# The loads of an inverse's 16x16 blocks, moved from ScalarE's queue to SyncE's and spread over units of dense products

## The chip, the cores and the metric

One NeuronCore of one Trainium2 chip runs the whole kernel. The engines are TensorE (PE in the profile; PEld is its weight load), VectorE (DVE), ScalarE (ACT), GpSimd (POOL) and SyncE (SP); each works through its own instruction queue in order, and DMAs are issued from the queues of SyncE and ScalarE. The metric is the device time of one execution in microseconds (us), lower is better.

## The reference

A decoder trunk of two layers on 256 tokens of width 2048. In each layer the normalised input goes through one wide input projection, whose columns feed two groups of heads: a gated DeltaNet (8 heads) and an HGRN2 recurrence (8 heads). Both outputs are joined, projected back and added; then a gated layer embedding is added.

```python
hn = rms_norm(h, norm_w[l])
proj = hn @ w_in[l]
...
y_a = deltanet_branch(dn_qkv, dn_z, dn_b, dn_a, ...)
y_b = hgrn2_branch(hg_q, hg_f, hg_i, hg_z, ...)
h = h + jnp.concatenate([y_a, y_b], axis=-1) @ w_out[l]
gate = jax.nn.sigmoid(h @ w_ple_gate[l])
h = h + (p[l] @ w_ple_up[l]) * gate
```

The DeltaNet needs, per head and chunk, a triangular system to be solved:

```python
A = jnp.where(strict, jnp.einsum("bhncd,bhnsd->bhncs", k_beta, k) * decay, 0.0)
sol = lax.linalg.triangular_solve(A + eye, rhs, left_side=True, lower=True, unit_diagonal=True)
```

The change touches only how the inverse of that unit triangular matrix is brought together.

## The kernel before

**Dense products.** Every projection runs as a sequence of steps. A step takes a block of weights of 512 KB (in0, in1, out, gate and up in the profile; the digit is the layer), multiplies both halves of the tokens with it, and ends with a call of `tick()`. One such step is a unit. Weights are f32 and are split into a high and a low part, with three matmuls for each product: `raw` is loaded by SyncE (line 378), ScalarE makes the high part `whi` (line 400), VectorE subtracts to get the low part `wlo` (line 402). There are three raw buffers (`WRAW = 3`) and three of each part. `ahead(n)` issues loads up to four steps ahead and splits up to two steps ahead of step n. The order of TensorE's instructions is that of the program text; the framework may shift instructions of the other engines against each other.

**Everything else is generators.** The work on heads is written as generators that are resumed by `tick()`: `yield self.wait(x)` lets so many units pass, `yield self.after(x)` or a lambda waits for a condition. How many units each wait takes stands in the tables `DELAY` (by kind: "d" DeltaNet group, "i" inverse, "h" HGRN2 group, "b" what follows the output and gate products) and `DELAY_AT` (for one group or layer: `d3c` is group 3's wait `c`, `i0t16` layer 0's wait `t16`). There are four groups of two heads each; in the profile dn03 is layer 0's DeltaNet group 3, hg11 layer 1's HGRN2 group 1. When a chunk of the input projection ends, ScalarE copies its PSUM bank with the row factor (`evict`, line 597, for instance hg01fqet), and a generator goes on from there. The dense products have three PSUM banks, a chunk uses two.

**The inverse** (class `Inverse`, di0 and di1 in the profile) does all 16 matrices of a layer at once, when the last of four groups has given its part (`given`). It clears the result `Tt` on GpSimd, collects the 16x16 diagonal blocks through DRAM with one matrix per partition, and inverts them with 15 short steps on VectorE (lines 653 and 656). Then ScalarE writes them to the DRAM scratch `d2` (line 658), two units pass (`w`), and eight loads of 16 KB each bring the blocks to the diagonals of `Tt` (line 662), one for each block row. After a further wait (`T`) VectorE transposes blocks of 32 (line 671), and three rounds of small TensorE products with copies between them join blocks of 16, 32 and 64 into one of 128, each round behind waits of its own (`t16`, `p16`, `t32`, `p32`, `t64`, `p64`; VectorE lines 690, 695, 718 to 721, ScalarE lines 681, 704, 712, 731, 740). At the end `ready` is set; the DeltaNet groups wait for it before `z0` and then multiply with `Tt`. The lines that the change touches:

```python
nc.scalar.dma_start(out=d2.rearrange("(q a c) -> q a c", q=128, a=16), in_=X)
yield self.wait("w")
for j in range(8):
    b = slice(16 * j, 16 * j + 16)
    nc.scalar.dma_start(out=Tt[b, :, b], in_=d2.rearrange("(i b a c) -> b a i c", i=NT, b=8, a=16)[j])
yield self.wait("T")
```

Of the kernel before, what the change touches and what calls it, by code (L numbers as in the profile page):

```python
# [15 lines left out]
DEPTH, D, T, KT = 2, 2048, 256, 16  # L16
# [15 lines left out]
def chunk_cols(chunk):  # L32

    return [(START[k], 16) if k == "ba" else (START[k] + 256 * g, 256) for k, g in chunk]
# [2 lines left out]

DELAY = {
    "d": {'c': 1, 'D': 4, 'k': 6, 'q': 7, 'ssq': 1, 'v': 5, 'z0': 1, 'S': 1, 'w': 1, 'z1': 1, 'o': 1, 'y': 3, 'yp': 1},
    "i": {'F': 4, 'F2': 1, 'F3': 1, 'F4': 1, 'w': 2, 'T': 6, 't16': 3, 'p16': 2, 't32': 3, 'p32': 2, 't64': 3, 'p64': 2},  # L40
    "b": {'o': 1, 'g': 4},
    "h": {'c': 1, 'f': 1, 'x2': 1, 'x4': 1, 'x8': 1, 'a': 2, 'x16': 1, 'x32': 1, 'x64': 1, 'u16': 2, 'u64': 1, 'o': 2, 'y': 2, 'yp': 1, 'q': 0},
}
# [1 line left out]
DELAY_AT = {  # L45
    "b1g": 5,
    "d0q": 6, "d0y": 2, "d0z1": 2,
    "d2D": 3, "d2k": 4, "d2o": 2, "d2q": 9, "d2y": 2,
    "d3D": 5, "d3ssq": 3,
    "h0o": 4, "h0u16": 1, "h0u64": 3, "h0y": 3, "h0yp": 2,  # L50
    "h1c": 3, "h1o": 1, "h1q": 1, "h1x32": 3, "h1x8": 3, "h1yp": 4,
    "h2c": 2, "h2f": 2, "h2q": 2,
    "h3u64": 2, "h3x2": 2,
    "i0p16": 1, "i0t16": 5,
    "i1t16": 2,
# [111 lines left out]
def trunk(ctx: ExitStack, tc: tile.TileContext, head, xT, x, pT, W, par, fw, cst, msk, eye, out):  # L167
    nc = tc.nc
# [113 lines left out]
    d2 = dr.tile([256 * 128], F32, name="d2")  # L282
# [20 lines left out]
    def bc1(ap, n):  # L303
        return ap.unsqueeze(1).to_broadcast([ap.shape[0], n, ap.shape[1]])
# [259 lines left out]
    def mix(tag, n, bufs, name):  # L564
        return mp.tile([128, n], F32, tag=tag, name=name, bufs=bufs)

    def v4(ap):
        return ap.rearrange("p (a b) -> p a b", b=128)
# [43 lines left out]
    class Inverse:  # L612


        NT = 4 * NG
# [21 lines left out]
        def run(self):  # L637
            n, Bt, NT = self.n, self.Bt, self.NT


            Tt = self.Tt = v4(mix("Tt", 128 * NT, 1, n + "Tt"))
# [3 lines left out]
            F, X = fx[:, 0], fx[:, 1]  # L645
# [3 lines left out]
            for c in range(1, 16):  # L649
# [3 lines left out]
                i = V.tensor_tensor(pr_[:, :c, :c], X[:, :c, :c], bc1(F[:, :c, c], c), ALU.mult)  # L653
# [5 lines left out]
            yield self.wait("w")  # L659
            for j in range(8):  # L660
                b = slice(16 * j, 16 * j + 16)
                nc.scalar.dma_start(out=Tt[b, :, b], in_=d2.rearrange("(i b a c) -> b a i c", i=NT, b=8, a=16)[j])
            yield self.wait("T")


# [4 lines left out]
            for b in blocks:  # L670
                i = V.transpose(Tn[b:b + 32], Tt[b:b + 32, :, b:b + 32])
# [52 lines left out]
            for i in range(NT):  # L724
                for b in (64, 96):
                    c = 64 * (i % 8)
# [7 lines left out]
            for i in range(NT):  # L734
                for b in (0, 32):
                    c = 64 * (i % 8)
# [520 lines left out]
    for l in range(DEPTH):  # L1257
# [25 lines left out]
        for c, k4 in order:  # L1283
# [5 lines left out]
            w = 2 if sum(n for _, n in chunk_cols(ch)) > 272 else 4  # L1289
# [114 lines left out]
```

## Time and profile before

| | |
|---|---|
| median of 3 runs | 1256.43 us (1256.11 to 1256.9) |
| the profiled execution | 1256.09 us |
| its span, first to last instruction | 1254.4 us |
| mean granted TensorE clock | 0.995 |
| waits of SyncE's queue for wlo before a weight load | 815.2 us, 299 times |

The difference of 1.7 us between the profiled execution's time and its span lies before the first and behind the last instruction. In the rows of the trace, times are us from the span's start, durations of single instructions us or, in groups, busy us and mean ns of one; a bracket at the end names the idle time before an instruction and what ended it. SPq and ACTq are DMA issues in the queues of SyncE and ScalarE.

### The profile page before, as it was taken

What the parts mean: (1) busy time and instruction counts of PE and PEld (TensorE: products, weight loads), DVE (VectorE), ACT (ScalarE), POOL (GpSimd) and SP (SyncE); (2) the same over time, 40 slices, a digit from 0 to 9 for tenths busy, and PEclk for the clock granted to TensorE, in tenths of its full rate; (3) what the DMA queues carried; (4) which work ended last, traced back from release to release, by engine and by line L of the source; (5) the groups of instructions that cost most, each with busy time, mean ns of one, the idle gap of its engine ahead of it and who ended that gap; (6) DMA issues with size and microseconds to landing.
All of it is one profiled execution on the core that took longest, in us unless ns stands there. A gap on an engine that the chain in (4) does not pass through costs nothing.

```text
span 1254.4 us, 21620 instructions
## 1 busy us (share of the span) xinstructions
PE 1232.5 (98%) x8385; PEld 1034.9 (83%) x8385; DVE 878.6 (70%) x1520; ACT 779.7 (62%) x1397; POOL 68.5 (5%) x64
## 2 busy tenths in 40 slices
PE   9999998999999999999999999989999999999996
PEld 7888887798888888888888888877988888888886
DVE  7777795968668656547667887877776695565566
ACT  7676765676657744447656777566776676444464
POOL 0310000000000100000003100000000000000010
PEclk9999999999999999999999999999999999999998
DMA  8555555545564455555655655645454546555563
GB/s 276 184 178 172 172 173 146 167 134 171 168 218 152 169 178 182 185 192 181 190 182 167 181 159 173 193 120 160 132 164 154 179 145 198 196 183 182 184 202 135
DMA packets 73719, 218.71 MB, mean 174 GB/s; under 512 B 15504, under 2 KB 20752, under 8 KB 73616
## 3 DMA queue, kind: packets, MB, share of 16 engines
q1 hardware_dynamic: 59040, 211.52, 52.6%
q10 hardware_dynamic: 14576, 5.80, 1.7%
q8 instruction: 66, 1.08, 0.3%
q14 instruction: 37, 0.30, 0.1%
HBM read 212.84 MB, written 4.46 MB: 173 GB/s over the span
## 4 chain that ended last, share of the span: by engine, by line
PE 83%; DVE 10%; ACT 2%; issue 2%; DMA 2%; ACTq 0%; SPq 0%; DVEq 0%
PE out L336 14%; PE gate L336 14%; PE in0dk L336 7%; PE in0dv L336 6%; PE in1dk L336 6%; PE in1hf L336 5%; PE in0hf L336 5%; PE in1dv L336 5%; PE in0hi L336 4%; PE in1hi L336 4%; DVE wlo L402 3%; PE up L336 2%; PE in1dz L336 1%; ACT whi L400 1%; PE in0dz L336 1%
## 5 line engine op out<-in xcount | busy, mean ns | idle before, releaser
L402 DVE TENSOR_TENSOR wlo<-raw,whi 128x1024 fp32r<-128x1024 f32 (+1 forms) x392 | 482.1, 1232 | 288.4 <-ACT whi L400 287.6
L400 ACT ACTIVATE whi<-raw 128x1024 fp32r<-128x1024 f32 (+1 forms) x392 | 411.6, 1052 | 333.5 <-PE out L336 89.6
L336 PE MATMUL in1hi<-whi,n1hi 128*128 128x512 f32 x128 | 52.3, 408 | 2.3 <-ACT hg11fqet L597 2.3
L336 PE MATMUL in1hf<-wlo,n1hi 128*128 128x512 f32 x128 | 50.0, 391 | 2.7 <-issue 1.4
L336 PE MATMUL in1dk<-whi,n1hi 128*128 128x512 f32 x128 | 51.2, 400 | 0.0
L336 PE MATMUL in1hf<-whi,n1hi 128*128 128x512 f32 x128 | 51.2, 400 | 0.0
L336 PE MATMUL in1dk<-wlo,n1hi 128*128 128x512 f32 x128 | 50.0, 391 | 0.7 <-DVE wlo L402 0.7
L336 PE MATMUL in1hi<-whi,n1lo 128*128 128x512 f32 x128 | 50.4, 393 | 0.0
L336 PE MATMUL in1hi<-wlo,n1hi 128*128 128x512 f32 x128 | 50.2, 392 | 0.0
L336 PE MATMUL gate<-whi,g0hi 128*128 128x512 f32 x128 | 50.1, 392 | 0.0
L336 PE MATMUL in1dk<-whi,n1lo 128*128 128x512 f32 x128 | 50.0, 391 | 0.0
L336 PE MATMUL in1hf<-whi,n1lo 128*128 128x512 f32 x128 | 49.9, 390 | 0.0
L336 PE MATMUL gate<-whi,g0lo 128*128 128x512 f32 x128 | 49.8, 389 | 0.0
L336 PE MATMUL gate<-wlo,g0hi 128*128 128x512 f32 x128 | 49.8, 389 | 0.0
L336 PE MATMUL in1dv<-whi,n1hi 128*128 128x512 f32 (+1 forms) x128 | 48.2, 377 | 0.0
L336 PE MATMUL in1dv<-whi,n1lo 128*128 128x512 f32 (+1 forms) x128 | 46.6, 364 | 0.0
L336 PE MATMUL in1dv<-wlo,n1hi 128*128 128x512 f32 (+1 forms) x128 | 46.5, 363 | 0.0
L336 PE MATMUL gate<-whi,g1hi 128*128 128x512 f32 (+1 forms) x120 | 45.5, 379 | 0.0
L336 PE MATMUL gate<-wlo,g1hi 128*128 128x512 f32 (+1 forms) x120 | 45.4, 379 | 0.0
L336 PE MATMUL gate<-whi,g1lo 128*128 128x512 f32 (+1 forms) x120 | 45.4, 378 | 0.0
L336 PE MATMUL in0hi<-whi,n0hi 128*128 128x512 f32 x96 | 38.6, 402 | 0.0
L336 PE MATMUL in0hf<-whi,n0hi 128*128 128x512 f32 x96 | 38.4, 400 | 0.0
(1495 smaller groups left out, 3174.8 us busy)
## 6 DMA issues: line engine op xcount, KB each, us to landing
raw<-W SPq DMA_DIRECT2D x384, 512.0 KB, 3.5
raw<-W SPq DMA_DIRECT2D x7, 544.0 KB, 4.2
h<-x SPq DMA_DIRECT2D x4, 512.0 KB, 4.6
xt<-xT SPq DMA_DIRECT2D x3, 512.0 KB, 6.6
out_dram<-h SPq DMA_DIRECT2D x6, 256.0 KB, 2.2
di0d<-di0Bt ACTq DMA_DIRECT2D x4, 256.0 KB, 2.8
di1d<-di1Bt ACTq DMA_DIRECT2D x4, 256.0 KB, 2.3
fw<-fw ACTq DMA_DIRECT2D x2, 512.0 KB, 4.2
```

The costliest lines, as they stand in the source:

```text
L336: return tc.keep_in_program_order(nc.tensor.matmul(*a, **k))
L400: S.activation(hi[:, sl], raw[:, sl], AF.Copy)
L402: V.tensor_tensor(lo[:, sl], raw[:, sl], hi[:, sl].bitcast(F32), ALU.subtract)
```

## The change

The eight loads of the 16x16 blocks are issued by SyncE rather than ScalarE, and one unit (`b`) passes after each. The wait `T` behind them becomes two units rather than six. Six other waits change by one or two units: `d2ssq` from 1 to 2, `d3D` from 5 to 3, `d3c` from 1 to 2, `h0q` from 0 to 1, `h1yp` from 4 to 3, `h2q` from 2 to 3. Of these, `c` stands between the copy of a chunk and its transposes on TensorE, `D` before the products of the decay, `ssq` before the row sums of q, `q` before the first factors of an HGRN2 group, `yp` before the transposes of its output. No instruction of arithmetic is added or removed.

```diff
-    "i": {'F': 4, 'F2': 1, 'F3': 1, 'F4': 1, 'w': 2, 'T': 6, 't16': 3, 'p16': 2, 't32': 3, 'p32': 2, 't64': 3, 'p64': 2},
+    "i": {'F': 4, 'F2': 1, 'F3': 1, 'F4': 1, 'w': 2, 'b': 1, 'T': 2, 't16': 3, 'p16': 2, 't32': 3, 'p32': 2, 't64': 3, 'p64': 2},
...
-    "d2D": 3, "d2k": 4, "d2o": 2, "d2q": 9, "d2y": 2,
-    "d3D": 5, "d3ssq": 3,
-    "h0o": 4, "h0u16": 1, "h0u64": 3, "h0y": 3, "h0yp": 2,
-    "h1c": 3, "h1o": 1, "h1q": 1, "h1x32": 3, "h1x8": 3, "h1yp": 4,
-    "h2c": 2, "h2f": 2, "h2q": 2,
+    "d2D": 3, "d2k": 4, "d2o": 2, "d2q": 9, "d2ssq": 2, "d2y": 2,
+    "d3D": 3, "d3c": 2, "d3ssq": 3,
+    "h0o": 4, "h0q": 1, "h0u16": 1, "h0u64": 3, "h0y": 3, "h0yp": 2,
+    "h1c": 3, "h1o": 1, "h1q": 1, "h1x32": 3, "h1x8": 3, "h1yp": 3,
+    "h2c": 2, "h2f": 2, "h2q": 3,
...
             for j in range(8):
                 b = slice(16 * j, 16 * j + 16)
-                nc.scalar.dma_start(out=Tt[b, :, b], in_=d2.rearrange("(i b a c) -> b a i c", i=NT, b=8, a=16)[j])
+                nc.sync.dma_start(out=Tt[b, :, b], in_=d2.rearrange("(i b a c) -> b a i c", i=NT, b=8, a=16)[j])
+                yield self.wait("b")
             yield self.wait("T")
```

## The prediction

> **What bounds the kernel now.** I read the page first (shares of busy time, then the costliest groups), then busy time by stage, then the chain of work inside the one stage where TensorE stops, then single instructions on both sides of each stop.
>
> ```profile
> span 1254.4 us, 21620 instructions
> PE 1232.5 (98%) x8385; PEld 1034.9 (83%) x8385; DVE 878.6 (70%) x1520; ACT 779.7 (62%) x1397; POOL 68.5 (5%) x64
> L402 DVE TENSOR_TENSOR wlo<-raw,whi 128x1024 fp32r<-128x1024 f32 (+1 forms) x392 | 482.1, 1232 | 288.4 <-ACT whi L400 287.6
> L400 ACT ACTIVATE whi<-raw 128x1024 fp32r<-128x1024 f32 (+1 forms) x392 | 411.6, 1052 | 333.5 <-PE out L336 89.6
> ```
>
> TensorE is idle for 1254.4 - 1232.5 = 21.9 us of the whole span, so with its matmuls unchanged nothing can be won beyond that idle time and slow matmuls. The stages (columns: length, PE, PEld, DVE, ACT, POOL, granted clock, DMA share, GB/s) say where it lies:
>
> ```profile
> 150.00:196.00 46.00, 46.00 (x387) 37.73 (x386) 38.85 (x91) 28.70 (x53) 1.82 (x1) 1.00 0.57 181
> 196.00:210.00 14.00, 10.69 (x49) 8.86 (x48) 6.36 (x10) 8.15 (x18) 0.00 (x0) 0.88 0.42 117
> 210.00:290.00 80.00, 79.59 (x1189) 68.06 (x1187) 65.61 (x124) 55.23 (x94) 1.56 (x1) 1.00 0.47 147
> 813.00:830.00 17.00, 14.74 (x70) 12.30 (x69) 8.74 (x12) 10.47 (x21) 0.00 (x0) 0.90 0.43 116
> 830.00:900.00 70.00, 67.25 (x1005) 57.30 (x1005) 52.24 (x102) 46.11 (x81) 1.29 (x1) 1.00 0.45 142
> ```
>
> Two stages, one in each layer, lose 14.00 - 10.69 = 3.31 us and 17.00 - 14.74 = 2.26 us, at a granted clock of 0.88 and 0.90 where the neighbours have 1.00. Two more lose 0.41 and 2.75 us at full clock. The chain in the first of these places:
>
> ```profile
> 188.90 3.71 DMA d<-di0fx
> 192.63 4.88 DMA di0Tt<-d
> ...
> 197.95 0.15 ACT whi L400
> ...
> 198.91 0.68 ACT hg01fqet L597
> ```
>
> The inverse writes its 16x16 blocks to DRAM, reads them back with the eight loads of line 662, and only then does ScalarE make a weight half (whi) and copy the PSUM bank (hg01fqet) for which TensorE waits. ScalarE waits because it issues those loads itself, and its queue is in order:
>
> ```profile
> 192.63 5.21 ACTq L662 DMA_DIRECT2D di0Tt<-d  x8
> 197.95 1.06 ACT L400 ACTIVATE whi<-raw 128x1024 fp32r<-128x1024 f32 x1 [7.28 <-DMA di0Tt<-d]
> 811.35 4.05 ACTq L662 DMA_DIRECT2D di1Tt<-d  x8
> 815.50 1.06 ACT L400 ACTIVATE whi<-raw 128x1024 fp32r<-128x1024 f32 x1 [6.22 <-DMA di1Tt<-d]
> ```
>
> It does no work for 7.28 us (6.22 in the second layer): first it waits for the DRAM write to land, then it issues for 5.21 (4.05) us.
>
> **What goes: the stall.** One row on either side of each stop, and two rows for the unhindered pace:
>
> ```profile
> 195.93 0.39 PE L336 MATMUL in0hi<-whi,n0alo 128*128 128x512 f32 x1
> 199.63 0.50 PE L336 MATMUL in0hi<-whi,n0ahi 128*128 128x512 f32 x1 [3.31 <-ACT hg01fqet L597]
> 203.97 0.48 PE L336 MATMUL in0hi<-whi,n0ahi 128*128 128x512 f32 x1
> 814.53 0.39 PE L336 MATMUL in1hi<-whi,n1lo 128*128 128x512 f32 x1
> 817.18 0.50 PE L336 MATMUL in1hi<-whi,n1hi 128*128 128x512 f32 x1 [2.26 <-ACT hg11fqet L597]
> 821.53 0.48 PE L336 MATMUL in1hi<-whi,n1hi 128*128 128x512 f32 x1
> 272.05 1.34 PE hg01po L336 x12
> 523.92 2.72 PE gate L336 x12
> ```
>
> From the last matmul before the stop to the first dense one after the small group hg00po lie 203.97 - 195.93 = 8.04 us, in layer 1 821.53 - 814.53 = 7.00 us. In between stand one dense matmul before the stop, six after it and the twelve of the small group. Unhindered they take 7 x 2.72/12 = 1.59 and 1.34 us, 2.93 together. So the stops cost 8.04 - 2.93 = 5.11 and 7.00 - 2.93 = 4.07 us, **9.18 us** in all; 3.31 + 2.26 of that is idle time and the other 3.6 is matmuls at a lower clock behind it. I take all of it as gone, since the profile names no second wait there: the bank that hg01fqet copies is complete when TensorE stops, the weights of that step are already there, and of ScalarE's work the stages show only 8.15 of 14.00 us. [...]
>
> **What comes: eight issues on SyncE.** SyncE also issues every weight load (raw), in order, each as soon as the subtraction (wlo) has freed one of three buffers:
>
> ```profile
> 190.03 0.33 SPq L378 DMA_DIRECT2D raw<-W  x1
> 190.70 1.22 DVE L402 TENSOR_TENSOR wlo<-raw,whi 128x1024 fp32r<-128x1024 f32 x1 [0.70 <-ACT whi L400]
> 191.95 0.33 SPq L378 DMA_DIRECT2D raw<-W  x1
> L662 ACTq DMA_DIRECT2D di0Tt<-d x8: 309/470/1202, 192.6 to 197.5; - x8
> di0Tt<-d ACTq DMA_DIRECT2D x8, 16.0 KB, 3.8
> raw<-W SPq DMA_DIRECT2D x384, 512.0 KB, 3.5
> ```
>
> An issue of a block load takes 0.47 us in the middle and 1.20 at most on ScalarE's queue; none is shown on SyncE's, where a weight load takes 0.33. I take 0.47, the row for the same transfer; the ends are 0.33 and 1.20. Behind each block load on SyncE wait only weight loads, and for these ScalarE's whi. Their room: three buffers turn over in three steps, 3 x 2.72 = 8.16 us, and need 3.5 (to landing) + 1.05 (whi) + 1.23 (wlo) = 5.8, which leaves 2.4 us before ScalarE is late at all, and then the weights prepared ahead are used up first. So 0.47 is hidden, and 1.20 too. The first load also waits for the DRAM write: it would stand in SyncE's queue behind the load at 190.03 and hold the next until 192.63 + 0.47 = 193.1 instead of 191.95, 1.2 us late, under 2.4. Cost 0; if that cover is gone, up to 1.2 us per layer.
>
> **What moves: the inverse.** Before, six units lay between the loads and the first transpose of the blocks; now eight and two, so everything after is 4 units later, 4 x 2.72 = 10.9 us, and where d3c holds the last head group back by one, 5 units. Its end has room: the last piece is written at 263.8 and first read at 295.3, more than twice the 13.6 us of five units.
>
> ```profile
> L740 ACT COPY di0Tt<-di0px x2: 578/579/580, 263.0 to 263.8; 64x512 f32<-64x512 f32 x2
> L336 PE MATMUL dn00pz<-dn00R,di0Tt x8: 272/275/275, 295.3 to 310.5; 128*128 128x128 f32 x8
> L671 DVE STREAM_TRANSPOSE di1T<-di1Tt 32x512 f32<-32x512 f32 x4 | 2.8, 700 | 0.1
> L690 DVE COPY_PREDICATED di1Tt<-ms,di1px 32x256 f32<-32x256 int32 x4 | 1.8, 444 | 0.1
> L695 DVE STREAM_TRANSPOSE di1T<-di1Tt 32x512 f32<-32x512 f32 x2 | 1.4, 702 | 0.0
> 846.60 0.50 PE L336 MATMUL in1hf<-wlo,n1hi 128*128 128x512 f32 x1 [1.32 <-DVE wlo L402]
> ```
>
> On VectorE the move puts 2.8 us of transposes (L671) into the stretch that ends at 846.60, where TensorE waits 1.32 us for a wlo, and takes 1.8 + 1.4 us (L690, L695) out of it: about -0.4 us, so I book 0. The bounds: below nothing, that wait and layer 0's 0.41 us close, -1.7; above, the transposes stand in the way undiluted, +2.8 per layer. The other edited delays (d2ssq, d3D, d3c, h0q, h1yp, h2q) add no instruction and shift steps by one or two units in stages where TensorE has no idle time; each is booked at 0, hidden by the weights prepared ahead, and could at worst open a stop like the 1.32 us one.
>
> **Sum.** 9.18 - 0 = 9.2 us off the profiled execution, which took 1256.09 us (1.7 us more than its span): 1246.9. The median of the three runs, 1256.43, is 0.3 us higher, so **1247.2 us**.
>
> **Rivals.**
> First, **the shifted inverse stands in the way**: 2.8 us of transposes come into VectorE's full stretch undiluted in one layer, and a 1.32 us wait opens besides. For it speaks that VectorE is busy 65.61 of 80.00 us there; against it the 3.2 us that leave. 1247.2 + 4.1 = 1251.3 us.
> Second, **the stop stays**: the DRAM write (line 658) remains on ScalarE, which waits there for VectorE's last reduction, and with the inverse starting a unit later the PSUM copy is held by that instead. It decides if that reduction ends later than about 195.5 (the copy of 0.68 us must be done when TensorE reaches 196.2); today the write is issued at 188.90, so 6.6 us would have to be lost, and a unit is 2.72. All 9.2 us back: 1256.4 us.
> Third, **slower: SyncE stands still at each block load** for H us, say until the one before has landed. A step gives it 2.72 us, of which 0.33 go to the weight load, so weights fall behind from H = 2.4, over eight steps by 8(H - 2.4) less the room of 2.4 us. That eats the 4.6 us won per layer from H = 3.3. At the 3.8 us of landing in layer 0 it is 8 x 1.4 - 2.4 = 8.8 us a layer: 1247.2 + 17.6 = 1264.8 us. Against it: on ScalarE eight issues fit into 5.21 us, so none waited for a landing. [...]
>
> **How the numbers follow.** The forecast gets 0.60, with a range of its own from 1245.5 (both VectorE waits close) to 1249.5 (one late weight load in each layer, 2 x 1.2); the first rival 0.18, the second 0.09, the third 0.08, and 0.05 goes to a time below 1245.5. The range for 8 in 10 goes from 1244.1 (1245.5 less the 2.75 - 1.32 = 1.4 us of idle time in the stage 830 to 900 that I left untouched) to 1252.5, one 1.2 us delay above the first rival. A measurement of this kernel tells about 0.2% (2.5 us) from no change, so faster means below 1253.9: 0.60 + 0.18 + 0.05 = 0.83; same 0.09; slower 0.08.
>
> **What would show it.** In the changed profile: no ACT row waiting 6 to 7 us for the block loads; the first in0hi and in1hi matmuls after a chunk change without a wait, and a granted clock of 1.00 in those stages; TensorE idle near 16 us instead of 21.9; eight SyncE rows for line 662 per layer, about 2.7 us apart, each 0.3 to 0.5 us, and ScalarE's waits for raw no longer than before. I am wrong if ScalarE waits for weights in that stretch (third rival), if hg01fqet still releases in0hi (second), or if new wlo waits follow the moved transposes (first).

## The result and the profile after

The changed kernel takes 1246.53 us (median of 4 runs, 1244.64 to 1248.62) against 1256.27 us (4 runs). The ratio is 0.9926 with a 95% interval of 0.9909 to 0.9942: faster by 0.6 to 0.9%. The prediction was 1247.2 us, with a range of 1244.1 to 1252.5. The four runs took 1244.64, 1244.89, 1248.17 and 1248.62 us; the profiled execution is that of 1248.17 us. Its page:

```profile
span 1246.4 us, 21626 instructions
PE 1229.5 (99%) x8385; PEld 1033.1 (83%) x8385; DVE 880.0 (71%) x1520; ACT 778.1 (62%) x1397; POOL 69.5 (6%) x64
```

The span is 8.0 us shorter. TensorE's idle time went from 21.9 to 1246.4 - 1229.5 = 16.9 us, which is 5.0 us; the other 3.0 us are busy time (1232.5 to 1229.5). About 2.0 us of these are matmuls that no longer run at a lower clock: behind the two stops of the kernel before (granted clock 0.76 from 199 to 206 and from 817 to 824) they cost 3.6 us, behind the one longer stop that is left (below; 0.83 from 216 to 226) 1.6 us. The remaining 1.0 us was not traced. The two stages of the stops, by the view of busy time (length, PE, PEld, DVE, ACT, POOL, granted clock, DMA share, GB/s):

```profile
196.00:210.00 14.00, 14.00 (x75) 11.91 (x74) 7.90 (x13) 8.10 (x19) 0.00 (x0) 1.00 0.71 215
813.00:830.00 17.00, 17.00 (x89) 14.36 (x88) 12.35 (x20) 12.51 (x25) 0.00 (x0) 1.00 0.63 186
```

Both are full at a clock of 1.00: the stops of 3.31 and 2.26 us are gone. The changed kernel has shorter ones later (matmuls of the timeline that TensorE waited for; the bracket is the idle time):

```profile
218.51 0.50 PE L336 MATMUL in0hi<-wlo,n0hi 128*128 128x512 f32 x1 [1.95 <-DVE wlo L402]
...
833.31 0.50 PE L336 MATMUL in1hi<-wlo,n1hi 128*128 128x512 f32 x1 [0.66 <-DVE wlo L402]
...
848.20 0.41 PE L336 MATMUL hg11pa<-hg11q,hg11k 128*32 128x48 f32 x18 [1.04 <-issue]
...
853.30 0.50 PE L336 MATMUL in1hf<-whi,n1hi 128*128 128x512 f32 x1 [0.91 <-issue]
```

The first two are new. The last two have no releaser in the trace, and the kernel before had one of that kind, of 1.43 us at 861.87, which is gone. So are the waits for wlo that it had (0.41 us at 233.51 and 1.32 at 846.60). SyncE's queue in the same place, with its issues in order of time:

```profile
188.04 2.36 SPq L378 DMA_DIRECT2D raw<-W  x2
193.01 1.32 SPq L662 DMA_DIRECT2D di0Tt<-d  x3
194.43 1.08 SPq L378 DMA_DIRECT2D raw<-W  x1
195.55 0.43 SPq L662 DMA_DIRECT2D di0Tt<-d  x1
196.08 0.39 SPq L378 DMA_DIRECT2D raw<-W  x1
196.51 0.92 SPq L662 DMA_DIRECT2D di0Tt<-d  x2
197.53 0.39 SPq L378 DMA_DIRECT2D raw<-W  x1
```

The loads do not stand one unit apart. The framework placed three in a row, because it moves instructions of every engine but TensorE, and SyncE waited with them from the weight load that ended at 190.4 until the DRAM write had landed, at 193.0. The next three weight loads followed at 194.43, 196.08 and 197.53. ScalarE then waits for weights:

```profile
198.86 1.06 ACT L400 ACTIVATE whi<-raw 128x1024 fp32r<-128x1024 f32 x1 [2.64 <-DMA raw<-W]
201.70 1.06 ACT L400 ACTIVATE whi<-raw 128x1024 fp32r<-128x1024 f32 x1 [1.78 <-DMA raw<-W]
```

### The profile page after: what moved, and what is told of

Its sections match the earlier page's. It is cut to its first block, busy times and chain, and to the rows that moved or that the text cites. A ratio compares the mean times of both kernels' runs of the same rounds, so it can differ in the third digit from the quotient of the medians.

```text
span 1246.4 us, 21626 instructions
## 1 busy us (share of the span) xinstructions
PE 1229.5 (99%) x8385; PEld 1033.1 (83%) x8385; DVE 880.0 (71%) x1520; ACT 778.1 (62%) x1397; POOL 69.5 (6%) x64
## 4 chain that ended last, share of the span: by engine, by line
PE 89%; DVE 6%; ACT 2%; DMA 1%; issue 1%; SPq 0%; DVEq 0%; ACTq 0%
PE out L336 14%; PE gate L336 14%; PE in1hf L336 7%; PE in0dk L336 7%; PE in0dv L336 6%; PE in1dv L336 6%; PE in1dk L336 6%; PE in1hi L336 6%; PE in0hf L336 5%; PE in0hi L336 4%; DVE wlo L402 2%; PE up L336 2%; PE in1dz L336 1%; PE in0dz L336 1%; ACT whi L400 1%
## 5 line engine op out<-in xcount | busy, mean ns | idle before, releaser
L336 PE MATMUL in0hi<-wlo,n0hi 128*128 128x512 f32 x96 | 38.3, 399 | 2.0 <-DVE wlo L402 2.0
```

What stands on the lines that cost most here:

```text
L336: return tc.keep_in_program_order(nc.tensor.matmul(*a, **k))
```

## The experiments

Three questions were open: whether the gain is the standstill of ScalarE or the new order of the work; whether SyncE or the spreading removes it; and what makes the new stop at 218.5. Ratios are to the kernel before, run on the same chip.

| kernel | us, median | ratio | 95% interval |
|---|---|---|---|
| changed kernel | 1246.53 | 0.9926 | 0.9909 to 0.9942 |
| loads at once, SyncE, old waits | 1250.19 | 0.9958 | 0.9946 to 0.9970 |
| loads spread, ScalarE | 1245.77 | 0.9924 | 0.9912 to 0.9936 |
| loads spread, SyncE, old six waits | 1247.29 | 0.9936 | 0.9924 to 0.9948 |
| SyncE in program order | 1245.70 | 0.9930 | 0.9916 to 0.9944 |
| SyncE in program order, pairs, later | 1245.15 | 0.9910 | 0.9896 to 0.9923 |
| pairs, ScalarE | 1252.05 | 0.9967 | 0.9955 to 0.9980 |
| four transposes kept in order | 1246.64 | 0.9923 | 0.9910 to 0.9935 |
| late but at once, ScalarE | 1256.64 | 1.0015 | 1.0005 to 1.0025 |

### Only the queue

```diff
 (kernel before)
-                nc.scalar.dma_start(out=Tt[b, :, b], ...)
+                nc.sync.dma_start(out=Tt[b, :, b], ...)
```

> The kernel before with one edit: the eight block loads are issued by SyncE, still all at once and with all waits as before. Theory A (ScalarE's standstill at line 662 is what TensorE waited for, 9.2 us in two places): both stops at the chunk change go, ScalarE shows no wait for the block loads. SyncE now stands still instead, from the weight load before to the landing of the DRAM write and eight issues (about 3 + 8 x 0.44 = 6.5 us); 2.4 us of that have room, so weights come some 4 us late in each layer, partly covered by the weights prepared ahead: 1247 to 1252 us. Theory B (the gain comes from the new order of the work, that is from the changed waits, not from the queue): no gain, 1255 to 1257 us.

1250.19 us: a gain, but 5.3 rather than 9.7 us, with no wait changed. The stops at the chunk change are gone, and each layer has another one a few us later. The matmuls that waited, and ScalarE's row ahead of the first:

```profile
205.97 1.11 PE L339 MATMUL hg00yp<-cs,hg00yt 128*128 128x128 f32 x4 [1.52 <-DVE hg00yt L575]
...
820.73 1.12 PE L339 MATMUL hg10yp<-cs,hg10yt 128*128 128x128 f32 x4 [1.76 <-DVE hg10yt L575]
```

```profile
201.22 1.06 ACT L400 ACTIVATE whi<-raw 128x1024 fp32r<-128x1024 f32 x1 [1.17 <-DMA raw<-W]
```

```profile
189.96 0.33 SPq L378 DMA_DIRECT2D raw<-W  x1
192.65 2.16 SPq L662 DMA_DIRECT2D di0Tt<-d  x3
...
197.37 0.39 SPq L378 DMA_DIRECT2D raw<-W  x1
```

SyncE issues no weight load between 189.96 and 197.37 us. ScalarE, in order, waits at 201.22 for such a load in the middle of the sums for hg00's output, so hg00yt comes late. Theory A's forecast holds, theory B's (no gain) does not. Eight loads at once on SyncE still make a standstill there, but a cheaper one.

### Spread, but on ScalarE

```diff
 (changed kernel)
-                nc.sync.dma_start(out=Tt[b, :, b], ...)
+                nc.scalar.dma_start(out=Tt[b, :, b], ...)
                 yield self.wait("b")
```

> The changed kernel with one edit: the block loads stay on ScalarE, one unit apart, all waits as in the changed kernel; TensorE's and VectorE's order is exactly that of the changed kernel. Theory A: ScalarE waits once for the DRAM write (about 2 us) and then gives 0.47 us to a load now and then, which its free time covers; the stops shrink to at most 1 us each and SyncE's hold goes: 1245 to 1249 us. Rival (the loads must leave ScalarE's queue, spreading is not enough): both stops come back with their slow matmuls, 1253 to 1257 us.

1245.77 us, all of the gain. ScalarE's rows between the landing of the DRAM write and the second PSUM copy, and what is left of the stop:

```profile
192.94 0.34 ACTq L662 DMA_DIRECT2D di0Tt<-d  x1
193.31 0.37 ACT L1104 COPY hg00Ax<-hg00pa 128x256 f32<-128x256 f32 x1 [2.11 <-DMA d<-di0fx]
193.33 2.01 ACTq L662 DMA_DIRECT2D di0Tt<-d  x2
195.46 1.06 ACT L400 ACTIVATE whi<-raw 128x1024 fp32r<-128x1024 f32 x1 [1.78 <-PE in0hf L336]
195.48 1.22 ACTq L662 DMA_DIRECT2D di0Tt<-d  x2
196.43 0.67 ACT L597 ACTIVATE hg01fqet<-in0hf,s0rt 128x512 f32<-128x512 f32 x1
```

```profile
197.15 0.50 PE L336 MATMUL in0hi<-whi,n0ahi 128*128 128x512 f32 x1 [0.47 <-ACT hg01fqet L597]
...
218.76 0.50 PE L336 MATMUL in0hi<-wlo,n0hi 128*128 128x512 f32 x1 [0.66 <-DVE wlo L402]
```

Five of the eight loads still stand ahead of the copy hg01fqet, with other work between them, and the stop shrinks from 3.31 to 0.47 us. SyncE was not needed; the rival falls.

### The six other waits put back

```diff
 (changed kernel)
-    "d2D": 3, "d2k": 4, "d2o": 2, "d2q": 9, "d2ssq": 2, "d2y": 2,
-    "d3D": 3, "d3c": 2, "d3ssq": 3,
+    "d2D": 3, "d2k": 4, "d2o": 2, "d2q": 9, "d2y": 2,
+    "d3D": 5, "d3ssq": 3,
...
```

> The changed kernel with the six other waits (d2ssq, d3D, d3c, h0q, h1yp, h2q) put back; SyncE, one unit apart, T of 2 stay. Theory A books these waits at nothing: 1245 to 1249 us, the stops stay away. Theory B: they carry the gain, 1251 to 1256 us.

1247.29 us. The interval overlaps that of the changed kernel, so no gain from the six waits can be told from none. Its profile has other small stops, one of them with no releaser in the trace:

```profile
220.73 0.50 PE L336 MATMUL in0hf<-wlo,n0ahi 128*128 128x512 f32 x1 [0.82 <-DVE wlo L402]
...
233.94 0.36 PE L336 MATMUL hg01pa<-hg01X 128*32 128x16 f32 x18 [2.59 <-issue]
```

### Spread over fewer units, and late but at once

The first takes a unit after every second load and so lets the inverse go on where it did before (ScalarE's queue). The second has the changed kernel's other waits and its late inverse, but all eight loads at once on ScalarE.

```diff
 (changed kernel, nc.scalar)
+                if j % 2:
                     yield self.wait("b")
```

```diff
 (changed kernel, nc.scalar)
-    'w': 2, 'b': 1, 'T': 2,
+    'w': 2, 'b': 1, 'T': 10,
...
-                yield self.wait("b")
```

> The kernel with the loads on ScalarE as in e2_spread_scalar, but a unit after every second load: 2 + 4 + 2 = 8 units, so the inverse goes on where it did in the kernel before, only the loads are spread. Theory A (standing still at the issues is the whole cost, when the inverse goes on costs nothing): ScalarE's waits at line 662 stay under 3 us a layer, 1245 to 1249 us. Rival (the gain needs the inverse to be four units later): the waits for wlo near 233 and 846 of the kernel before return, 1249 to 1254 us.

> The changed kernel with its six other waits and the inverse as late as there (2 + 10 units instead of 2 + 8 + 2), but the eight loads on ScalarE and all at once, as before. Theory A (only the issues in one go ahead of the PSUM copies cost): both stops of 2 to 3 us at hg01fqet and hg11fqet are back, 1253 to 1257 us. Theory B (the new order of the work gains, wherever the loads stand): 1245 to 1250 us.

The pairs give 1252.05 us. Theory A's 1245 to 1249 us were missed. The rival's number came, but not by its mechanism: the waits for wlo near 233 and 846 are not back, the old stops are.

```profile
198.97 0.50 PE L336 MATMUL in0hi<-whi,n0ahi 128*128 128x512 f32 x1 [2.97 <-ACT hg01fqet L597]
...
816.77 0.50 PE L336 MATMUL in1hi<-whi,n1hi 128*128 128x512 f32 x1 [2.88 <-ACT hg11fqet L597]
```

```profile
193.26 3.11 ACTq L662 DMA_DIRECT2D di0Tt<-d  x4
196.48 1.06 ACT L400 ACTIVATE whi<-raw 128x1024 fp32r<-128x1024 f32 x1 [2.86 <-issue]
196.50 1.68 ACTq L662 DMA_DIRECT2D di0Tt<-d  x2
198.23 1.27 ACT L597 ACTIVATE hg01fqet<-in0hf,s0rt 128x512 f32<-128x512 f32 x2 [0.70 <-DMA di0Tt<-d]
```

The framework put all eight loads ahead of hg01fqet, four of them in a row. Yet the kernel gains 4.2 us (1256.26 to 1252.05 on that chip) with stops as long in sum as before (5.85 against 5.57 us). TensorE's idle time is 1250.3 - 1232.2 = 18.1 us against 21.9: the two waits for wlo (0.41 and 1.32 us) and the one with no releaser (1.43 us) are closed. So part of the changed kernel's gain does not hang on the stops; which of the remaining edits closes these waits was not tried. Late but at once gives 1256.64 us, no gain at all, with stops of 5.61 and 4.04 us:

```profile
201.92 0.79 PE L336 MATMUL in0hi<-whi,n0ahi 128*128 128x512 f32 x1 [5.61 <-ACT hg01fqet L597]
...
820.74 0.80 PE L336 MATMUL in1hi<-whi,n1hi 128*128 128x512 f32 x1 [4.04 <-ACT hg11fqet L597]
```

```profile
193.85 6.07 ACTq L662 DMA_DIRECT2D di0Tt<-d  x8
199.96 0.37 ACT L1103 COPY hg00Ax<-hg00pa 128x256 f32<-128x256 f32 x1 [9.10 <-DMA di0Tt<-d]
```

Everything else of the change is in place here, so theory B falls as the explanation of the whole gain. The new order does save something: these stops are 4.1 us longer than those of the kernel before (9.65 against 5.57 us), and the time is only 1.6 us longer (1256.64 against 1255.05 on that chip).

### The new stop at 218.5

Theory C blames the weight loads held behind the first block loads on SyncE, theory D the transposes of the inverse in VectorE's full stretch. Three kernels: SyncE's DMAs pinned to the program's order (the first block load then comes two weight loads earlier); the same with the loads later and in pairs, so that the DRAM write has long landed; and all four transposes pinned.

```diff
 (changed kernel; the first three lines in load())
-        if n <= 17:
-            tc.keep_in_program_order(i)
+        tc.keep_in_program_order(i)
...
-                nc.sync.dma_start(out=Tt[b, :, b], ...)
+                tc.keep_in_program_order(nc.sync.dma_start(out=Tt[b, :, b], ...))
```

```diff
 (the same, and)
-    'w': 2, 'b': 1, 'T': 2,
+    'w': 6, 'b': 1, 'T': 2,
...
+                if j % 2:
                     yield self.wait("b")
```

```diff
 (changed kernel)
                 i = V.transpose(Tn[b:b + 32], Tt[b:b + 32, :, b:b + 32])
-                if b == 0:
-                    tc.keep_in_program_order(i)
+                tc.keep_in_program_order(i)
```

> The changed kernel with SyncE's DMAs kept in the order of the program text, so that the loads really stand one at a time between weight loads; the first of them then comes two weight loads earlier in SyncE's queue than in the changed kernel, where three come in a row. Theory C (the 1.95 us wait that the changed kernel has at 218.5 comes from weight loads that stand behind the first block load until the DRAM write lands): SyncE is held longer, ScalarE's waits for raw grow from 17 us, TensorE gets new stops of 2 to 6 us a layer: 1249 to 1256 us. Rival D (that wait comes from the transposes of line 672 moved into VectorE's full stretch; SyncE's hold is covered): 1245 to 1248.5 us, as the changed kernel.

> The changed kernel with SyncE's DMAs in the order of the program text, w of 6 units and a unit after every second load: the loads come four units later and in pairs, when the DRAM write has long landed, and the transposes behind them keep their place (6 + 4 + 2 units = 2 + 8 + 2). Theory C (SyncE's hold makes most of the 1.95 us stop at 218.5): SyncE no longer waits for the DRAM write, ScalarE's waits for raw fall from 17 us to under 8, the stop shrinks to 0.7 us or less: 1244 to 1246 us with a narrow spread. Theory D (the transposes of line 672 in VectorE's full stretch make it): the stop stays near 1 to 2 us, 1245 to 1248.5 us.

> The changed kernel with all four transposes of line 672 kept in the order of the program text (it kept one of them; three had been put forward between the first steps of the next HGRN2 group). TensorE's order stays. Theory D: 2.1 us of VectorE's work leave the stretch ahead of 218.5, the stop there goes in both layers (0.66 us in layer 1) with its slow matmuls: 1243 to 1245.5 us. Theory C: the stop keeps more than 1 us, 1245 to 1248.5 us.

*Program order* did not follow theory C's forecast. SyncE waits 7.0 us for the DRAM write in either layer (waits of SyncE's queue; in the changed kernel 2.5 and 1.8 us), yet the median is 1245.70 us and the stop in layer 0 is 1.05 us:

```profile
SPq L661 <- DMA d<-di0fx: 7.0, 1, 7.0
SPq L661 <- DMA d<-di1fx: 7.0, 1, 7.0
```

```profile
219.02 0.50 PE L336 MATMUL in0hi<-wlo,n0hi 128*128 128x512 f32 x1 [1.05 <-DVE wlo L401]
```

The profiled execution took 1250.08 us, while four of the six runs lie at 1245.3 to 1245.74 us (the two others at 1250.08 and 1250.27). It has a stop of 1.73 us with no releaser that ends at 848.49, and around it the granted clock falls, to 0.51 from 848 to 855. The others were not profiled, so it is not shown that this makes the 4.4 us:

```profile
848.00:855.00 7.00, 6.51 (x127) 5.51 (x127) 4.87 (x14) 0.00 (x0) 0.00 (x0) 0.51 0.26 87
```

SyncE's issues in layer 0:

```profile
192.09 0.39 SPq L378 DMA_DIRECT2D raw<-W  x1
192.54 0.42 SPq L661 DMA_DIRECT2D di0Tt<-d  x1
193.06 0.40 SPq L378 DMA_DIRECT2D raw<-W  x1
193.50 0.42 SPq L661 DMA_DIRECT2D di0Tt<-d  x1
194.02 0.40 SPq L378 DMA_DIRECT2D raw<-W  x1
```

After the hold only one block load stands between two weight loads, and three of these are out by 194.4, in the changed kernel by 197.9. So the length of the wait is not the measure. How soon SyncE catches up behind it would fit layer 0, a reading made after the fact, but not layer 1: there three weight loads are out by 808.6 instead of 813.9, and the stop is 1.14 instead of 0.66 us. *Pairs, later* is as theory C has it: the stop is 0.32 us in both layers, with the transposes where they were, and ScalarE's waits for raw are 8.8 us in all, near the 8 that theory C had asked for.

```profile
217.05 0.50 PE L336 MATMUL in0hi<-wlo,n0hi 128*128 128x512 f32 x1 [0.32 <-DVE wlo L401]
...
830.04 0.50 PE L336 MATMUL in1hi<-wlo,n1hi 128*128 128x512 f32 x1 [0.32 <-DVE wlo L401]
```

*Transposes kept* does take them out of the stretch ahead of the stop, and in layer 0 it stays, 0.87 and 1.55 us in two parts; theory D's forecast fails there. The test is not clean, since the weight load behind the hold also came later, at 196.19 instead of 194.43. In layer 1 the stop shrinks from 0.66 to 0.43 us.

```profile
215.08 0.49 PE L336 MATMUL in0hi<-whi,n0hi 128*128 128x512 f32 x1 [0.87 <-ACT whi L400]
217.13 0.80 PE L336 MATMUL in0hi<-wlo,n0hi 128*128 128x512 f32 x1 [1.55 <-DVE wlo L402]
```

So the block loads on SyncE most likely make most of the 1.95 us stop: it is 0.66 us with the loads on ScalarE and 0.32 us with SyncE's wait gone (in a kernel that differs by the pinned order and the pairs too). This is not settled. Layer 1 of the changed kernel has the same three loads in a row behind a wait (808.57 to 809.88) and a stop of only 0.66 us, as with the loads on ScalarE. "Pairs, later" has the lowest median of all, 1245.15 us, on another chip, but its interval overlaps that of the changed kernel, so it is not shown to be better.

### The changed kernel once more

> The changed kernel once more, for a second profile; its runs so far lie at 1244.6 to 1244.9 and at 1248.2 to 1248.6 us, and the profile is of 1248.17 us. If the stop at 218.5 with the matmuls at a lower clock behind it makes the difference, a run near 1244.7 us shows that stop short (under 1 us) at a granted clock of 1.00; if the two levels have another cause, the stop is 1.9 us again.

The run took 1246.70 us. Its stop and the granted clock in the stretch from 216 to 226, first of this run, then of the first profile (the columns of the stage view above):

```profile
219.43 0.50 PE L336 MATMUL in0hi<-wlo,n0hi 128*128 128x512 f32 x1 [1.88 <-DVE wlo L402]
...
216.00:226.00 10.00, 8.12 (x36) 6.39 (x35) 10.00 (x20) 7.18 (x13) 0.00 (x0) 1.00 0.39 133
```

```profile
216.00:226.00 10.00, 8.05 (x29) 6.13 (x28) 9.24 (x18) 7.39 (x13) 0.00 (x0) 0.83 0.44 157
```

The run fell between the two levels, so the question was not put to the test that was planned. The stop is as long, but no clock drop follows. From the stop's end to the first in0hf matmul, eleven matmuls, it is 222.05 - 219.43 = 2.62 us here and 222.72 - 218.51 = 4.21 us in the first profile; the 1.6 us between them are about the 1.5 us between the two runs. Runs at 1244.7 us were not caught in a profile, and what they lack stays open.

## Why the prediction was right

**The stall goes, 9.18 us: right.** Both stages are full at clock 1.00. The prediction gave the move to SyncE as the means, and it is one: alone it takes these stops away and wins 5.3 us. Spreading one by one is another, on ScalarE's own queue, and wins the whole. On ScalarE's queue nothing is won with the loads late but at once, and in pairs the stops stay.

**The eight issues cost nothing: wrong by about one stop.** An issue took 0.43 us, near the 0.47 booked, and the first one did wait for the DRAM write. The step that failed is that only one block load would hold the next weight load, which would come 1.2 us late: three came in a row, the weight load that the prediction put at 193.1 came at 194.43, and two more late ones followed. The 2.4 us of room were not there either. They were worked out from the median landing of 3.5 us, but the weight loads issued at 196.08 and 197.53 took 5.5 and 5.7 us to land (in the kernel before, the one at 191.95 took 4.7), and ScalarE waited 1.26 us for weights at 191.99, before the hold could tell. Price, as far as the runs of the last question show it: a stop of 1.95 us, with 1.6 us of slow matmuls behind it in one of two profiles.

**The moved inverse costs nothing: not contradicted, but wrong in its picture.** Of the four transposes three did not move: first and last stand at

```profile
L672 DVE STREAM_TRANSPOSE di0T<-di0Tt x4: 692/702/708, 208.8 to 221.5; 32x512 f32<-32x512 f32 x4
```

where the kernel before had all of them from 208.3 to 210.5. What came later is everything behind them. The waits for wlo at 233.51 and 846.60 closed, -1.7 us, which the prediction had as the favourable bound of the move. That the move closed them is not shown: they are also gone in the kernel with pairs on ScalarE, where the transposes stand at 210.4 to 212.6. The end of the inverse had its room.

**The six other waits cost nothing: not contradicted,** within the interval of the kernel that puts them back.

**The sum.** Two terms are off in opposite directions: the late weight loads cost 1.95 us or, with the slow matmuls, about 3.5 us, and the waits that closed give back 1.7. The profiled execution, 1248.17 us, is 1.3 us above the 1246.9 forecast for it; that the median of four runs spread over 4 us came within 0.7 us of the forecast is partly luck. TensorE's idle time, forecast near 16 us, is 16.9.

**The rivals.** Of the forecast's signs of being wrong two came, though its time held: ScalarE waited for weights in that stretch (2.64 and 1.78 us), the third rival's sign, and a new wait for wlo of 1.95 us, the first rival's. The block loads did not come 2.7 us apart either. "SyncE stands still at each load" did not come about: issues follow each other in 0.5 us. "The stop stays" did not: hg01fqet releases no matmul any more. The shifted transposes are not shown to be the new wait's cause, since three of the four did not shift. Block loads on SyncE's queue are not needed for weights that land late: with them on ScalarE's queue, the weight loads issued at 199.91 and 201.19 also took 5.6 and 5.5 us to land, and in the kernel before those issued at 238.2 and 239.6, long after its last block load at 197.5, took 5.5 and 5.3. The median landing of a block load is 3.8 us in both layers (before, 3.8 and 2.5), and ScalarE's waits for raw are 17.3 us in all against 13.9. The wait in SyncE's queue for the DRAM write (2.5 us in layer 0) explains that the weight loads were issued late; no run separates late issue from late landing further.

## What to carry to other kernels

The issue of a block load took 0.47 us in the middle on ScalarE's queue (the kernel before) and 0.43 us on SyncE's (the changed kernel). Eight in a row behind a wait stopped ScalarE for 6.2 to 9.1 us, and the price was paid where a PSUM copy stood behind them: TensorE's stops of 2.26 to 5.61 us. Put other work between the issues before looking for another queue, and read the instruction order that the framework made, since a wait counted in units of the program text may not survive its reordering. The first block load waited on SyncE's queue for the DRAM write to land, 2.5 and 1.8 us in the changed kernel and 7.0 us in either layer in program order, and the next weight load stood behind it (issued at 194.43 in the changed kernel's layer 0). Issue such a load later, if there is room: in "pairs, later" SyncE's wait for the write was gone and the stop 0.32 us.

## What the hardware showed that was not expected

The granted clock fell after stops of 3.31, 2.26 and 1.95 us (0.76 from 199 to 206, 0.76 from 817 to 824, 0.83 from 216 to 226), and also after one of 1.76 us (820.73 in the kernel with only the queue changed; 0.57 from 822 to 826) and with one of 1.73 us (program order, 848.49; 0.51 from 848 to 855). It stayed at 1.00 after one of 1.88 us in the same place of the same program as the 1.95, and after 1.52 (205.97, only the queue changed; 196 to 212) and 1.32 us (846.60 in the kernel before; 846 to 852). So in these runs the length of a stop does not decide it alone; what else does was not shown. The matmuls at the lower clock behind the first three cost 1.6 to 1.8 us each time, as much as a short stop itself.

Short stops of 0.4 to 2.6 us with no releaser in the trace appear in most of these kernels among the small matmuls of an HGRN2 group (hg11pa, hg01pa) and behind them. Their cause was not tried.
